# Hybrid decoder trunk on one core: other places for the first token tiles, the first gate tile and the narrow projections

## The chip, the cores and the metric

The kernel runs on one core of one Trainium2 chip. The metric is the device time of one execution in microseconds (us). The engines are named as the profile names them: PE is TensorE's matmuls and PEld its weight loads, DVE is VectorE, ACT is ScalarE, POOL is GpSimd, SP issues DMAs. Matrix products land in PSUM, which has eight banks; everything else on the chip is SBUF.

## The reference, cut to what matters

The model is one layer: a mixer with two branches (gated linear attention, "gla", and "mlstm"), each with four heads, and a gated feed-forward block with a causal convolution. 16 learned tokens stand ahead of 1024 input tokens, so the sequence has T = 1040 rows of 1024 channels.

```python
h = concat([meta, x])                      # 1040 x 1024
n = rms_norm(h, norm_mix)
proj = n @ w_in + b_in                     # q, k, v, gate r, 16 low-rank columns for gla;
                                           # q, k, v, gate o, 4 + 4 columns (i, f) for mlstm; gates a, b
log_a = log_sigmoid(g_lr @ gla_w_gate + gla_b_gate) / 16
o_gla = head_rms(gla(q, k, v, log_a)) * silu(r)
o_ml  = head_rms(mlstm(conv(q, k), v, i, f)) * sigmoid(o)
h = h + (sigmoid(a) * (o_gla @ w_gla) + sigmoid(b) * (o_ml @ w_ml)) @ w_out
h = h + conv_ffn(rms_norm(h, norm_ffn))
return rms_norm(h, norm_final)[16:]
```

## The kernel before, in words

Every float32 product is made of three products of split operands: a matrix X is held as a rounded part XH and a rest XL, and XH·WH, XL·WH and XH·WL are summed in PSUM. Splitting costs one copy on ACT (the H part) and one subtraction on DVE (the L part).

**The token tiles.** `load_x` (line 291) loads tile 0 (the 16 meta tokens) and tiles 1 to 8 (128 tokens each) by SP into SBUF slots with tags "w" (tiles 0 to 4), "q" (5, 6) and "k" (7, 8), slots that the heads use later. `norm_x(i)` (line 299) takes a tile's sum of squares on ACT (L305), makes the reciprocal root on DVE and POOL (L308, L310), scales the tile by it and by the norm's vector `gmix` on DVE (L311), transposes it on PE in two groups of four (L316, PSUM tag "s", three banks) and splits it into xH (ACT, L318) and xL (DVE, L320). Lines 323 to 341 write out the order of these loads, norms and first weights by hand.

**The weights.** `Units` holds a list of weight pieces in the order of use. `get(u)` loads and splits the pieces up to two ahead of u (the first three without looking ahead). `prep` (line 96) loads a piece into one of two raw slots by SP, copies on ACT (L102) and subtracts on DVE (L103) into a ring of three slots each for H and L. Before, unit 0 is the key of head 0 (gk), 1 the query (gq) and 2 the narrow projections "lr": the 16 low-rank columns of gla and the 4 + 4 of mlstm, padded to 128 in two zeroed tiles that take one slot of each ring (line 106). `prep_small` loads them with three DMAs.

**The products.** `proj_cm` (line 146) multiplies a weight piece of 128 columns with the tokens, piece of tokens by piece: 24 products (8 blocks of channels, 3 each) into one of three PSUM banks with tag "pj", and then a copy out by ACT that adds the bias from `col`. `TH_ALL` and `TH_POST` cut the tokens into three pieces of some 342 ("thirds" below), `SEG_ALL` and `SEG_POST` into four of some 256, whose borders fall on token tiles. For head 0 the key, the query and lr go piece by piece in turn (`together`, line 403), so that products start with tiles 0 to 2. `proj_v` makes the values in nine pieces of 24 or fewer products. `columns()` (line 282) transposes the rows of biases and other vectors in `va` into `col`; it stands ahead of the last token tile. `conv_columns()` does the same for the feed-forward's convolution; it stands behind head 0's projections.

**The order after the start.** `main(gen)` runs the main work, and after each piece `advance()` runs one step of the side chain, up to its next `yield`. Stage s (lines 863 to 870) appends head s to the side chain (and `small_rows` behind head 0, which needs lr's rows), and then does as main work the gate projection of head s (two tiles, six thirds; copy out at L426), the key, query and value of head s + 1 (15 pieces) and one gate of the merge (three). A head's side chain ends with four pairs of chunks (L716 to L727) and `post` (line 510): a scale per token (L92, L520), the gate's activation (L518), transposes (L530, L537), the product with the gate tile (L532, L538), the split and two stores (L540 to L543), for each of two halves. The gate tiles have tag "r" with two slots, so that a gate tile of head s + 1 can be written only when `post` of head s has read the one before it.

**How an order comes about.** Each instruction has a priority, which is its place in the program; `hp(n)` moves it up by n places, though not ahead of `floor`, which is set behind the start. At compile time each engine's order is fixed from these priorities and from what is ready in the compiler's own model of time; on the chip each engine then works strictly in that order.

Of the kernel before, what the change touches and what calls it, by code (L numbers as in the profile page):

```python
# [16 lines left out]
P = 128  # L17
D = 1024
NM = 16
SEQ = 1024  # L20
T = NM + SEQ
NK = D // P
NP = SEQ + 2
T0 = NM - 2
NC = SEQ // P
# [19 lines left out]
def hybrid_kernel(ctx, tc, x, meta, norm_mix, w_in, b_in, gla_w_gate, gla_b_gate, gla_norm,  # L45
# [7 lines left out]
    def rowb(ap, off, n):  # L53
        return bass.AP(tensor=ap.tensor, offset=ap.offset + off, ap=[[0, P], [1, n]])
# [3 lines left out]
    def hp(n):  # L58

        return tc.high_priority(offset=max(1, min(n, tc.cur_priority - floor[0])))  # L60
# [42 lines left out]
        nc.vector.tensor_tensor(wL, raw, wH.bitcast(F32), OP.subtract)  # L103
        return wH, wL

    lrHL = [wp.tile([P, NK, P], F32R, name=f"w{p}_lr", tag="w" + p) for p in "HL"]
    for t in lrHL:
        nc.vector.memset(t.bitcast(F32), 0.0)
    SMALL = ((0, O_LR, 16), (32, O_MI, 4), (64, O_MF, 4))

    def prep_small():
# [92 lines left out]
    def u_cm(w, n0, name):  # L204
        return U.add(wsrc(w, 0, NK, n0, P), [P, NK, P], name)
# [7 lines left out]
    def head_units(s):  # L213
        h = s % 4
        if s < 4:
            uk[s], uq[s] = u_cm(w_in, O_GK + P * h, f"gk{h}"), u_cm(w_in, O_GQ + P * h, f"gq{h}")
            if s == 0:
                uk["lr"] = U.add()
            uv[s] = u_v(O_GV + DV * h, f"gv{h}_")
        else:  # L220
            uk[s], uq[s] = u_cm(w_in, O_MK + P * h, f"mk{h}"), u_cm(w_in, O_MQ + P * h, f"mq{h}")
            uv[s] = u_v(O_MV + DV * h, f"mv{h}_")

    def gate_units(s):
        h = s % 4
        o = (O_GR if s < 4 else O_MO) + DV * h
        ur[s] = [u_cm(w_in, o + P * j, f"r{s}_{j}") for j in range(2)]

    head_units(0)
    for s in range(8):  # L230
# [51 lines left out]
    def columns():  # L282

        tp = ps.tile([P, 512], F32, name="coltp", tag="s", bufs=3)
        nc.tensor.transpose(tp[:, :nrow], va[:nrow, :], ident[:nrow, :nrow])
        nc.vector.tensor_copy(col, tp[:, :nrow])
        nc.vector.tensor_scalar(col[:, C_GQ:C_GQ + 4], col[:, C_GQ:C_GQ + 4], QS, None, OP.mult)

    xts = []

    def load_x(*tiles):
        for i in tiles:
            n = NM if i == 0 else P
            tag, bufs = [("w", 5), ("q", 2), ("k", 2)][(i >= 5) + (i >= 7)]
            xt = hd.tile([P, T], F32, name=f"xt{i}", tag=tag, bufs=bufs)
            nc.sync.dma_start(xt[:n, :D], meta if i == 0 else x[P * (i - 1):P * i, :])
            xts.append(xt)

    def norm_x(i):
        n = NM if i == 0 else P  # L300
        c0 = 0 if i == 0 else NM + P * (i - 1)
# [3 lines left out]
        nc.scalar.activation(junk[:n, :D], xt[:n, :D], AF.Square, accum_out=ss[:n])  # L305
        with hp(40):
            v = hd.tile([P, 1], F32, name=f"xv{i}", tag="xv", bufs=3)
            nc.vector.tensor_scalar(v[:n], ss[:n], 1.0 / D, EPS, OP.mult, OP.add)  # L308
            rs = hd.tile([P, 1], F32, name=f"xr{i}", tag="xr", bufs=3)
            last = nc.gpsimd.tensor_tensor(rs[:n], v[:n], mhalf[:n], OP.pow)  # L310
        nc.vector.scalar_tensor_tensor(xt[:n, :D], xt[:n, :D], rs[:n], gmix[:n], OP.mult, OP.mult)  # L311
        for g in range(2):
            tp = ps.tile([P, 4, P], F32, name=f"xtp{i}_{g}", tag="s", bufs=3)
            for j in range(4):
                k = 4 * g + j
                nc.tensor.transpose(tp[:, j, :n], xt[:n, k * P:(k + 1) * P], ident[:n, :n])  # L316
            h4 = xH[:, 4 * g:4 * g + 4, c0:c0 + n]
            nc.scalar.activation(h4, tp[:, :, :n], AF.Copy)  # L318
            l4 = xL[:, 4 * g:4 * g + 4, c0:c0 + n]
            nc.vector.tensor_tensor(l4, tp[:, :, :n], h4.bitcast(F32), OP.subtract)  # L320
        return last

    load_x(0)
    nc.sync.dma_start(gmix, rowb(norm_mix, 0, D))
    load_x(1, 2)
    norm_x(0)
    norm_x(1)
    U.get(0, 0)
    load_x(3)
    U.get(1, 0)  # L330
    norm_x(2)
    load_x(4, 5)
    U.get(2, 0)
    norm_x(3)
    load_x(6, 7, 8)
    for dst, ap in small:
        nc.sync.dma_start(dst, ap)
    for i in range(4, NC + 1):
        if i == NC:
            columns()  # L340
        last = norm_x(i)
    for t, c in ((xH, 0), (xL, 32)):
        m3 = xM[:, :48 * NK].rearrange("p (k w) -> p k w", w=48)
        nc.scalar.activation(m3[:, :, c:c + NM], t[:, :, :NM].bitcast(F32), AF.Copy)
    floor[0] = tc.cur_priority

    fc = const.tile([P, 4, 44], F32, name="fc")

    def conv_columns():
        for i in range(2):  # L350
            tp = ps.tile([P, 512], F32, name=f"ftp{i}", tag="s", bufs=3)
            nc.tensor.transpose(tp[:, :88], vf[:, i, :], ident[:88, :88])
            nc.vector.tensor_copy(fc[:, 2 * i:2 * i + 2, :].rearrange("p a b -> p (a b)"), tp[:, :88])

    def cc(i):
        return col[:, i:i + 1]
# [32 lines left out]
    def head_proj(s):  # L389
        h = s % 4  # L390
        hh = heads[s] = {}
        bB = hd.tile([P, DV], F32, name=f"bB{s}", tag="bB", bufs=2)
        nc.sync.dma_start(bB, rowb(b_in, (O_GV if s < 4 else O_MV) + DV * h, DV))
        kT = hd.tile([P, T + 3], F32, name=f"kT{s}", tag="k", bufs=2)
        qT = hd.tile([P, T + 3], F32, name=f"qT{s}", tag="q", bufs=2)
        hh["k"], hh["q"] = kT, qT
        if s < 4:
            pk = proj_cm(uk[s], TH_ALL if s else SEG_ALL, 0, lambda p, t0, n: nc.scalar.activation(
                kT[:, t0:t0 + n], p, AF.Identity, bias=cc(C_GK + h)))
            pq = proj_cm(uq[s], TH_POST if s else SEG_POST, T0, lambda p, t0, n: nc.scalar.activation(  # L400
                qT[:, t0:t0 + n], p, AF.Identity, bias=cc(C_GQ + h), scale=QS))
            if s == 0:
                yield from together(pk, pq, proj_cm(uk["lr"], SEG_ALL, 0, lambda p, t0, n: nc.scalar.activation(
                    raw_s[0:96, t0:t0 + n], p[0:96, :], AF.Identity, bias=bsm[0:96])))
            else:
                yield from pk
                yield from pq
        else:
            for z, u, c in ((kT, uk[s], C_MK), (qT, uq[s], C_MQ)):
                nc.gpsimd.memset(z[:, 0:3], 0.0)  # L410
                yield from proj_cm(u, TH_ALL, 0, lambda p, t0, n, z=z, c=c: nc.scalar.activation(
                    z[:, 3 + t0:3 + t0 + n], p, AF.Identity, bias=cc(c + h)))
# [6 lines left out]
    def gate_proj(s):  # L419
        hh = heads[s]  # L420
        hh["r"] = []
        for j in range(2):
# [3 lines left out]
            yield from proj_cm(ur[s][j], TH_POST, T0, lambda p, t0, n, r=r, c=c: nc.scalar.activation(  # L426
                r[:, t0:t0 + n], p, AF.Identity, bias=cc(c)))

    def merge_gate(which, j):
# [427 lines left out]
    def main(gen):  # L857
        for _ in gen:
            advance()

    main(head_proj(0))
    conv_columns()
    for s in range(8):
        side.append((gla if s < 4 else mlstm)(s))
        if s == 0:
            side.append(small_rows())
        main(gate_proj(s))
        if s < 7:
            main(head_proj(s + 1))
        main(merge_gate("a", s))  # L870
# [565 lines left out]
```

## Time and profile before

| | |
|---|---|
| median of 3 runs | 1974.15 us (1971.41 to 1975.38) |
| profiled execution | 1973.3 us, of which the profile's span is 1971.4 us |
| PE busy | 1936.3 us, 98% of the span |
| DVE, ACT, POOL busy | 49%, 38%, 15% |
| DMA | 224.82 MB, mean 114 GB/s |

A row of the timeline gives start, duration, engine, line, operation, names (written <- read), the shapes, how many instructions are merged, and in brackets the idle time of the engine just before with what ended it. A row of the list of waits gives the waiting engine and line, whom it waited for, the total in us, how often and the longest. A row of the windows gives for each stretch its length and each engine's busy time with the number of instructions, then the granted clock of TensorE, the DMA engines' share and GB/s. The order of the engines there is PE, PEld, DVE, ACT, POOL. A busy time of PE includes the modelled end of a pipelined product, so that products follow each other closer than their durations say.

### The profile page before, as it was taken

The numbers are of one execution on the slowest core, as the hardware profiler recorded it, in microseconds if no ns is written. First come the engines' busy times: TensorE is split into PE (matmuls) and PEld (weight loads), VectorE is DVE, ScalarE is ACT, GpSimd is POOL, SyncE is SP. The second block draws the span as 40 slices with busy tenths as digits, with TensorE's granted clock in tenths as the row PEclk, the third lists the DMA queues.
The fourth block names the chain that finished last, engine by engine and source line by source line (L and its number), as shares of the span: only waits on it lengthen the run. The fifth ranks groups of instructions, "written<-read, shape, count | busy, mean of one in ns | idle before, by whom it ended". The sixth has DMA issues, their size and how long they took to land. (4 is left out here: it accounts for less than half of the span.)

```text
span 1971.4 us, 31346 instructions
## 1 busy us (share of the span) xinstructions
PE 1936.3 (98%) x13333; PEld 1854.0 (94%) x13333; DVE 963.4 (49%) x1427; ACT 744.3 (38%) x1176; POOL 286.5 (15%) x201
## 2 busy tenths in 40 slices
PE   7999999999999999999999999999999999999998
PEld 6999999999999999999999999999999999978886
DVE  6265263637535343422022446698888888710202
ACT  5145333535534343423221234544545444431211
POOL 2020020101000000000000002012222222364220
PEclk9999999999999999999999999999999999999999
DMA  4210403232234222226971433333333333487731
GB/s 152 57 33 23 100 22 95 37 70 69 61 96 90 64 88 63 79 62 123 315 268 54 150 108 108 124 102 126 116 119 123 118 118 113 170 301 263 239 101 43
DMA packets 191271, 224.82 MB, mean 114 GB/s; under 512 B 11102, under 2 KB 150640, under 8 KB 191131
## 3 DMA queue, kind: packets, MB, share of 16 engines
q1 hardware_dynamic: 190843, 221.76, 37.2%
q8 instruction: 105, 1.72, 0.4%
q10 hardware_dynamic: 288, 1.05, 0.1%
q14 instruction: 35, 0.29, 0.0%
HBM read 166.07 MB, written 56.71 MB: 113 GB/s over the span
## 5 line engine op out<-in xcount | busy, mean ns | idle before, releaser
L1323 PE MATMUL pd<-ringH,a 128*128 128x512 f32 x416 | 131.6, 393 | 1.5 <-DMA a<-adrL 1.5
L154 PE MATMUL pj<-xH,wH_r 128*128 128x342 f32 x384 | 124.2, 323 | 0.4 <-ACT r L426 0.4
L154 PE MATMUL pj<-xH,wL_r 128*128 128x342 f32 x384 | 122.9, 320 | 0.0
L154 PE MATMUL pj<-xL,wH_r 128*128 128x342 f32 x384 | 122.5, 319 | 0.0
L1357 DVE TENSOR_TENSOR acc<-pd,acc 128x512 f32<-128x512 f32 x16 | 11.1, 692 | 196.3 <-PE pd L1323 196.3
L1323 PEld LDWEIGHTS pd<-ringH,a 128*128 128x128 f32 x416 | 78.0, 188 | 19.6 <-DMA a<-adrL 2.0
L1323 PE MATMUL pd<-ringL,a 128*128 128x512 f32 x208 | 82.5, 397 | 1.5 <-POOL ringL L1302 1.5
L197 PE MATMUL pv<-wH_gv,xH 128*128 128x256 f32 x256 | 75.4, 294 | 0.0
L197 PE MATMUL pv<-wH_mv,xH 128*128 128x256 f32 x256 | 74.2, 290 | 0.0
L1193 PE MATMUL po<-wL_wo,yH 128*128 128x256 f32 x256 | 72.0, 282 | 2.0 <-DVE wL_wo L103 2.0
L1193 PE MATMUL po<-wH_wo,yH 128*128 128x256 f32 x256 | 72.8, 284 | 0.9 <-DVE h L1200 0.9
L154 PEld LDWEIGHTS pj<-xH,wH_r 128*128 128x128 f32 x384 | 72.2, 188 | 1.1 <-ACT r L426 0.5
L627 POOL TENSOR_TENSOR pk<-pk,kT 128x512 f32<-128x512 f32 x24 | 40.2, 1685 | 226.9 <-ACT pk L626 226.8
L197 PE MATMUL pv<-wL_gv,xH 128*128 128x256 f32 x256 | 72.7, 284 | 0.0
L197 PE MATMUL pv<-wH_gv,xL 128*128 128x256 f32 x256 | 72.6, 283 | 0.0
L154 PEld LDWEIGHTS pj<-xL,wH_r 128*128 128x128 f32 x384 | 72.2, 188 | 0.0
L154 PEld LDWEIGHTS pj<-xH,wL_r 128*128 128x128 f32 x384 | 72.2, 188 | 0.0
L197 PE MATMUL pv<-wL_mv,xH 128*128 128x256 f32 x256 | 71.9, 281 | 0.0
L197 PE MATMUL pv<-wH_mv,xL 128*128 128x256 f32 x256 | 71.9, 281 | 0.0
L1193 PE MATMUL po<-wH_wo,yL 128*128 128x256 f32 x256 | 71.8, 281 | 0.0
L1154 DVE SCALAR_TENSOR_TENSOR cv<-u,fc,cv 128x1024 f32<-128x1024 f32 x44 | 69.4, 1578 | 0.4
L201 DVE TENSOR_TENSOR v<-pv,bB 128x256 f32<-128x256 f32 x64 | 27.0, 421 | 78.1 <-PE pv L197 77.9
(618 smaller groups left out, 6714.5 us busy)
## 6 DMA issues: line engine op xcount, KB each, us to landing
rd<-in_ffn_w_down_dram SPq DMA_DIRECT2D x36, 512.0 KB, 5.9
rg<-in_ffn_w_up_dram SPq DMA_DIRECT2D x22, 512.0 KB, 4.2
ru<-in_ffn_w_up_dram SPq DMA_DIRECT2D x22, 512.0 KB, 3.8
a<-adrH SPq DMA_DIRECT2D x44, 256.0 KB, 5.0
a<-adrL SPq DMA_DIRECT2D x44, 256.0 KB, 4.7
adrH<-aH SPq DMA_DIRECT2D x21, 512.0 KB, 2.6
adrL<-aL SPq DMA_DIRECT2D x21, 512.0 KB, 2.6
wr_r<-in_w_in_dram SPq DMA_DIRECT2D x16, 512.0 KB, 4.0
```

The source lines that it names most:

```text
L154: nc.tensor.matmul(pt[:, :n], a[:, k, :], b[:, k, base + t0:base + t0 + n], start=(i == 0), stop=(i == 3 * NK - 1))
L197: nc.tensor.matmul(pt[:, :DV], a[:, k, t0:t0 + P], b[:, k % 4, :], start=(i == 0), stop=(i == 3 * NK - 1))
L201: nc.vector.tensor_tensor(vt[:n, c, :DV], pt[:n, :DV], bB[:n, :], OP.add)
L627: nc.gpsimd.tensor_tensor(pe, pe, lv(kv, b)[:, :, 0, :], OP.mult)
L1154: nc.vector.scalar_tensor_tensor(y, u[:, j:SEQ + j], fc[:, j, jj:jj + 1], y, OP.mult, OP.add)
L1193: nc.tensor.matmul(pt[:, :DV], a, b[:, k % 4, :], start=(k == 0 and i == 0), stop=(k == NK - 1 and i == len(terms) - 1))
L1323: nc.tensor.matmul(pts[t][n], a[:, c], b[:, 512 * n:512 * n + 512], start=start and i == 0, stop=stop and i == 2)
L1357: nc.vector.tensor_tensor(acc[:, h], pts[t][n], acc[:, h], OP.add)
```

## The change

- The first two token tiles are loaded ahead of `gmix`. Tile 3 is loaded behind the weights of gk and gq; five of the rows that `col` needs come behind it, four others go at the very top on ACT's own DMA queue, and the rest behind tile 8.
- `columns()` moves ahead of tile 3's norm, `conv_columns()` behind tile 8's.
- Unit 2 is now the first gate tile's weights (r0_0). Its projection takes the place of lr in `together`, in four pieces; lr follows behind it in thirds. In stage 0 only the second gate tile is left of the gate projection.
- The padded narrow weights lie in one tile in a slot of tag "v" and no longer in the weights' rings. Token tiles 5 and 6 share the other slot of "v", tile 7 has a slot of "k", tile 8 one of "q".
- Tile 1's transposes use the "pj" banks, and each tile's split (L318, L320) has a priority of 40.
- Eight products of the identity with itself, whose result nobody reads, stand at the top.

```diff
-    lrHL = [wp.tile([P, NK, P], F32R, name=f"w{p}_lr", tag="w" + p) for p in "HL"]
-    for t in lrHL:
-        nc.vector.memset(t.bitcast(F32), 0.0)
+    lr2 = hd.tile([P, 2, NK, P], F32R, name="w_lr", tag="v", bufs=2)
+    nc.vector.memset(lr2.bitcast(F32), 0.0)
+    lrHL = [lr2[:, i] for i in range(2)]
...
             if s == 0:
+                ur[0] = [u_cm(w_in, O_GR, "r0_0")]
                 uk["lr"] = U.add()
...
-            tag, bufs = [("w", 5), ("q", 2), ("k", 2)][(i >= 5) + (i >= 7)]
-            xt = hd.tile([P, T], F32, name=f"xt{i}", tag=tag, bufs=bufs)
+            if i in (5, 6):
+                if i == 5:
+                    x56.append(hd.tile([P, 2, D], F32, name="xt56", tag="v", bufs=2))
+                xt = x56[0][:, i - 5]
+            else:
+                tag, bufs = ("w", 5) if i < 5 else ("k", 2) if i == 7 else ("q", 2)
+                xt = hd.tile([P, T], F32, name=f"xt{i}", tag=tag, bufs=bufs)
...
-            tp = ps.tile([P, 4, P], F32, name=f"xtp{i}_{g}", tag="s", bufs=3)
+            tp = ps.tile([P, 4, P], F32, name=f"xtp{i}_{g}", tag="pj" if i == 1 else "s", bufs=3)
...
+            with hp(40):
+                h4 = xH[:, 4 * g:4 * g + 4, c0:c0 + n]
+                nc.scalar.activation(h4, tp[:, :, :n], AF.Copy)
+                l4 = xL[:, 4 * g:4 * g + 4, c0:c0 + n]
+                nc.vector.tensor_tensor(l4, tp[:, :, :n], h4.bitcast(F32), OP.subtract)
...
+    def idle_products(n, name):
+        pt = ps.tile([P, P], F32, name=f"idle{name}", tag="ot", bufs=2)
+        for _ in range(n):
+            nc.tensor.matmul(pt, ident, ident, start=True, stop=True)
+
+    idle_products(8, "a")
+    for dst, ap in small[:4]:
+        nc.scalar.dma_start(dst, ap)
+    load_x(0, 1)
+    nc.sync.dma_start(gmix, rowb(norm_mix, 0, D))
+    load_x(2)
+    norm_x(0)
+    norm_x(1)
+    U.get(0, 0)
+    U.get(1, 0)
+    norm_x(2)
+    load_x(3)
+    for dst, ap in small[4:9]:
+        nc.sync.dma_start(dst, ap)
+    load_x(4, 5)
+    U.get(2, 0)
+    columns()
+    norm_x(3)
+    load_x(6, 7, 8)
+    norm_x(4)
+    for dst, ap in small[9:]:
+        nc.sync.dma_start(dst, ap)
+    for i in range(5, NC + 1):
+        last = norm_x(i)
+    conv_columns()
...
-                yield from together(pk, pq, proj_cm(uk["lr"], SEG_ALL, 0, lambda p, t0, n: nc.scalar.activation(
-                    raw_s[0:96, t0:t0 + n], p[0:96, :], AF.Identity, bias=bsm[0:96])))
+                yield from together(pk, pq, gate_proj(0, (0,)))
+                yield from proj_cm(uk["lr"], TH_ALL, 0, lambda p, t0, n: nc.scalar.activation(
+                    raw_s[0:96, t0:t0 + n], p[0:96, :], AF.Identity, bias=bsm[0:96]))
...
-        main(gate_proj(s))
+        main(gate_proj(s, (0, 1) if s else (1,)))
```

The lines that the second part of the diff replaces (323 to 341 before) load tile 0, `gmix`, tiles 1 and 2, then norm tiles 0 and 1, get gk, load tile 3, get gq, norm tile 2, load tiles 4 and 5, get lr, norm tile 3, load tiles 6 to 8 and all the rows, and norm the rest.

More of the change, by code (lines that the diff above doesn't have):

```diff
@@ L226, in gate_units @@
         o = (O_GR if s < 4 else O_MO) + DV * h
-        ur[s] = [u_cm(w_in, o + P * j, f"r{s}_{j}") for j in range(2)]
+        ur.setdefault(s, []).extend(u_cm(w_in, o + P * j, f"r{s}_{j}") for j in range(len(ur.get(s, ())), 2))
     head_units(0)
@@ L287, in columns @@
         nc.vector.tensor_scalar(col[:, C_GQ:C_GQ + 4], col[:, C_GQ:C_GQ + 4], QS, None, OP.mult)
-    xts = []
+    xts, x56 = [], []
     def load_x(*tiles):
@@ L316, in norm_x @@
                 nc.tensor.transpose(tp[:, j, :n], xt[:n, k * P:(k + 1) * P], ident[:n, :n])
[L317 to L320, printed above, removed]
-        return last
[L323 to L345, printed above, removed]
+            with hp(40):
[3 more added lines that the diff above has]
+                nc.vector.tensor_tensor(l4, tp[:, :, :n], h4.bitcast(F32), OP.subtract)
+        return last
     fc = const.tile([P, 4, 44], F32, name="fc")
@@ L353, in conv_columns @@
             nc.vector.tensor_copy(fc[:, 2 * i:2 * i + 2, :].rearrange("p a b -> p (a b)"), tp[:, :88])
+    def idle_products(n, name):
[27 more added lines that the diff above has]
+    conv_columns()
+    for t, c in ((xH, 0), (xL, 32)):
+        m3 = xM[:, :48 * NK].rearrange("p (k w) -> p k w", w=48)
+        nc.scalar.activation(m3[:, :, c:c + NM], t[:, :, :NM].bitcast(F32), AF.Copy)
+    floor[0] = tc.cur_priority
     def cc(i):
@@ L417, in head_proj, with gate_proj @@
         yield from proj_v(uv[s], bB, vt)
-    def gate_proj(s):
+    def gate_proj(s, js=(0, 1)):
         hh = heads[s]
-        hh["r"] = []
-        for j in range(2):
+        hh.setdefault("r", [])
+        for j in js:
             r = hd.tile([P, NP], F32, name=f"r{s}_{j}", tag="r", bufs=2)
@@ L425, in gate_proj @@
             hh["r"].append(r)
-            yield from proj_cm(ur[s][j], TH_POST, T0, lambda p, t0, n, r=r, c=c: nc.scalar.activation(
+            yield from proj_cm(ur[s][j], TH_POST if s or j else SEG_POST, T0, lambda p, t0, n, r=r, c=c: nc.scalar.activation(
                 r[:, t0:t0 + n], p, AF.Identity, bias=cc(c)))
@@ L861, in hybrid_kernel @@
     main(head_proj(0))
-    conv_columns()
     for s in range(8):
```

## The prediction, made before the changed kernel ran

> **What bounds the kernel now.** I read the page first: busy shares, then the idle column of TensorE's groups, then the list of waits for that engine, and only then the start in order of time.
>
> ```profile
> PE 1936.3 (98%) x13333; PEld 1854.0 (94%) x13333; DVE 963.4 (49%) x1427; ACT 744.3 (38%) x1176; POOL 286.5 (15%) x201
> ```
>
> TensorE is busy 98% of 1971.4 us, so the time is its work plus its holes. The waits, and the 5 us windows of the start (the last three columns: granted clock, DMA share, GB/s), say where holes are. The fifth row is ScalarE's, and (f) needs it:
>
> ```profile
> PE xtp L316 <- DVE xt L311: 10.4, 2, 10.0
> PE ot L530 <- DVE or L520: 1.6, 1, 1.6
> PE pj L154 <- ACT r L426: 0.4, 1, 0.4
> PE pj L154 <- ACT kT L398: 0.4, 1, 0.4
> ...
> ACT r L426 <- DVE of L538: 32.6, 5, 10.9
> ...
> 5.00:10.00 5.00, 0.02 (x1) 0.02 (x1) 2.05 (x16) 2.30 (x4) 1.77 (x2) 1.00 1.03 367
> ...
> 15.00:20.00 5.00, 2.74 (x15) 2.07 (x16) 5.00 (x10) 4.95 (x11) 1.10 (x2) 0.83 0.87 236
> 20.00:25.00 5.00, 5.00 (x24) 5.00 (x24) 4.59 (x10) 2.79 (x5) 2.52 (x3) 0.50 0.34 124
> ```
>
> Ten microseconds pass before anything can be transposed, VectorE is full from 15 to 20, and from 20 to 25 TensorE runs at half the clock. After 37 us it hardly waits. So the change can win holes at the start, and lose where it makes new ones later; the work of TensorE stays. The first gate tile goes from three pieces to four and the narrow projection from four to three: 24 products more and 24 fewer over nearly the same columns, net nothing.
>
> **The start, step by step.** The rows that carry it:
>
> ```profile
> 1.26 0.41 SPq L324 DMA_DIRECT2D gmix<-in_norm_mix_dram  x1
> ...
> 7.36 1.06 ACT L305 ACTIVATE xj<-xt 128x1024 f32<-128x1024 f32 x1 [3.29 <-DMA xt<-in_x_dram]
> 8.65 1.27 DVE L311 SCALAR_TENSOR_TENSOR xt<-xt,xr,gmix 16x1024 f32<-16x1024 f32 x1
> ...
> 12.40 1.28 DVE L311 SCALAR_TENSOR_TENSOR xt<-xt,xr,gmix 128x1024 f32<-128x1024 f32 x1 [0.41 <-POOL xr L310]
> 16.00 1.27 DVE L311 SCALAR_TENSOR_TENSOR xt<-xt,xr,gmix 128x1024 f32<-128x1024 f32 x1
> 17.19 1.22 DVE L103 TENSOR_TENSOR wL_gq<-wr_gq,wH_gq 128x1024 fp32r<-128x1024 f32 x1
> 18.99 0.68 DVE L320 TENSOR_TENSOR xL<-xtp,xH 128x512 fp32r<-128x512 f32 x1
> 19.83 0.57 PE L154 MATMUL pj<-xL,wH_gk 128*128 128x272 f32 x1
> ...
> 24.74 0.43 PE L154 MATMUL pj<-xL,wH_gk 128*128 128x272 f32 x1
> ...
> 30.59 0.29 PE L154 MATMUL pj<-xH,wH_lr 128*128 128x272 f32 x1
> ...
> 32.98 0.28 PE L154 MATMUL pj<-xL,wH_lr 128*128 128x272 f32 x1
> 33.20 1.07 PE L316 MATMUL xtp<-ident,xt 128*128 128x128 f32 x8
> ```
>
> (a) Tile 1 lands at 7.36 behind gmix. 512 KB at 367 GB/s is 1.4 us, so with their places exchanged tile 1 lands near 5.9 and gmix near 7.4. VectorE's scaling (L311) needs both; it waited for tile 1's sum of squares until 8.65 and will wait for gmix: 1.3 us earlier. Tile 2's scaling follows (12.40 becomes about 11.1). Then comes the larger part: between 12.40 and the last low part of tile 2 (18.99, end 19.67) VectorE also did tile 3's scaling (1.27) and wL_gq (1.22). With a priority of 40 the low parts go ahead of these, and tile 1's transposes leave tag "s" for "pj", so tile 2 waits for no bank. 19.67 - 1.3 - 2.5 = 15.9; I take 16.3 for the first sustained product instead of 19.83, since ScalarE works in order and may stand behind the cast of gq, bounds 15.2 and 18. Of the 3.5 us, tile 3's eight transposes (1.1, the row at 33.20) fall back into the products' time: -2.4.
>
> (b) The first pieces of kT could not leave PSUM before `col` was made:
>
> ```profile
> 34.60 0.29 PE L154 MATMUL pj<-xH,wL_lr 128*128 128x272 f32 x1
> 35.70 0.25 DVE L286 COPY col<-coltp 128x98 f32<-128x98 f32 x1
> 36.43 0.48 ACT L398 ACTIVATE kT<-pj,col 128x272 f32<-128x272 f32 x1
> 36.96 0.39 PE L154 MATMUL pj<-xH,wH_gk 128*128 128x256 f32 x1 [0.39 <-ACT kT L398]
> ```
>
> From 34.9 to 36.96 TensorE had only eight transposes (1.1): 1.0 us lost. Moving columns() ahead of tile 3, with its rows loaded early, and tiles 5 and 6 out of the "q" slots, ends that: -1.0. Next late there would be r0_0's weights, in need near 16.3 + 48 products = 23 to 25. Their load has to wait for the raw slot of gk (until wL_gk is made) and holds tiles 6 to 8 behind it on SP; these are used at 33 or later. Bubbles from this and from VectorE's row: +0.5, bounds 0 and 1.5.
>
> (c) At the half clock a product took 0.23 us (19.83 to 24.74, 21 steps), at the full one 0.126 (30.59 to 32.98, 19 steps): 23 products, 2.4 us lost. After, the products meet the same gate; I take 1.7 lost, bounds 0 and 3.4: -0.7.
>
> (d) Costed at nothing: four row loads on ScalarE's queue. SP paid 0.41 for an issue, so 1.6 us on ScalarE, which idles 3.29 us before 7.36; without that cover 1.6. Five more row loads stand on SP ahead of tile 4, 2.1 us of issuing, but the DMA engines are full (share 1.03 from 5 to 10 us) and drain behind SP; without that cover 2.1. The narrow weights' loads and casts move behind the tiles, and lr now comes after twelve pieces of 24 products, some 35 us on; its tile in slot "v" is read out before v0's first sum. The eight idle products: a plain float32 one is two instructions, and eight took 2.05 us at full clock (row at 339.13 below), 4.1 at half. They run at the very top, where TensorE has nothing else for 10.0 us (the first wait above).
>
> By the trace the clock fell after 1.55 us of idleness (below), so idle products that end well before the first transposes carry nothing to 16. The Trainium skill ("TensorE: Matmul & The Clock Gate", Part 1, the HAM clock gate) has the clock at half until some 3.4 us of sustained work, and back at half after an idle window of that length. That agrees on the products; on the idle length the trace is stricter, and by that rule alone the clock's share in (f) would cost nothing and the sum would be 0.9 lower.
>
> Sum at the start: -2.4 - 1.0 + 0.5 - 0.7 = **-3.6**, ends +0.8 (18, cold 3.4, bubbles 1.5) and -6.9 (15.2, no cold).
>
> **What the missing gate tile does to the order.** After each third of main work (24 products of 342 columns, or one v piece) one step of the side chain is issued. Stage 0 had 24 main steps (gate 6, next head 15, merge 3); after, 21. By their yields gla needs 23 side steps and small_rows 7, so everything up to head 3 comes three main steps later against main.
>
> (e) In stage 0 this helps:
>
> ```profile
> 183.36 1.93 DVE L520 TENSOR_SCALAR or<-or,rs0r 128x256 f32<-128x256 f32 x7 [1.19 <-POOL rs0r L92]
> 183.77 1.12 PE L530 MATMUL ot<-ident,or 128*128 128x128 f32 x4 [1.55 <-DVE or L520]
> ...
> 173.35:182.22 8.87, 8.87 (x74) 8.64 (x72) 6.46 (x5) 8.71 (x12) 2.82 (x2) 1.00 0.00 1
> 182.22:183.77 1.55, 0.00 (x0) 0.00 (x1) 0.41 (x2) 0.74 (x1) 1.10 (x1) 1.00 0.00 0
> 185.56:188.97 3.41, 3.41 (x19) 3.41 (x17) 3.28 (x7) 1.06 (x1) 0.00 (x0) 0.50 0.02 5
> ```
>
> Three v pieces (8.87 us) covered a chain of 10.4 and TensorE stood 1.55; then the clock was half for 3.41 us, 1.7 lost. After, one v piece and two thirds of ga stand there, 3.0 + 2 x 3.6 = 10.2 (a third's 3.6 comes under (f)): 0.2 is left and the clock stays, **-3.0**, or 0 if not.
>
> (f) At the start of stage 2 it hurts. A tile r2_0 takes the slot of r1_0, and its copies out of PSUM wait for head 1's post (L538):
>
> ```profile
> 308.07 0.59 PE L721 MATMUL op<-S,qh 128*128 128x256 f32 x2
> ...
> 312.51 2.56 DVE L520 TENSOR_SCALAR or<-or,rs1r 128x256 f32<-128x256 f32 x8 [1.79 <-POOL rs1r L92]
> 315.25 1.21 DVE L103 TENSOR_TENSOR wL_gk<-wr_gk,wH_gk 128x1024 fp32r<-128x1024 f32 x1
> 319.80 0.60 PE L530 MATMUL ot<-ident,or 128*128 128x128 f32 x4
> 324.01 0.60 PE L530 MATMUL ot<-ident,or 128*128 128x128 f32 x4
> 324.65 0.75 DVE L532 SCALAR_TENSOR_TENSOR of<-ot,col,r 128x512 f32<-128x512 f32 x1 [3.45 <-PE ot L530]
> 326.45 0.21 DVE L538 SCALAR_TENSOR_TENSOR of<-otm,col,r 128x2 f32<-128x2 f32 x1
> 326.72 0.22 PE L537 MATMUL otm<-ident,om 2*128 2x2 f32 x1 [0.61 <-DVE of L538]
> 326.75 1.42 ACT L426 ACTIVATE r<-pj,col 128x342 f32<-128x342 f32 x3 [1.65 <-DVE of L538]
> 339.13 2.05 PE L564 MATMUL sc<-qT,kT 128*128 128x128 f32 x16 [0.17 <-DVE of L532]
> ```
>
> Before, four thirds lay between the last chunk pair (308.7) and L538 (326.45), and all three "pj" banks were full: it just fitted, with 0.61 + 0.4 us of holes. After, one third is left there (two of r2_0 are done already). Without main work in its way the chain takes from 308.7 to 316.5 (scaling and wL_gk), two L532 and L538 (1.7), the copy out (0.55): 10.1 us. The cover is one third (4.21 from one group of transposes to the next, less 0.60: 3.6), sixteen transposes (2 x 1.1) and two small ones (0.4): 6.2. A hole of 3.9, 2.9 more than now. 1.7 for the clock counts half, since the transposes break the hole up: **+3.7**, bounds 0 (the scheduler fills it) and 7.0 (a chain of 12.5, the clock in full). Behind the waiting copies ScalarE holds the cast for head 1's second half, which L538 there needs 13 us later, as now.
>
> (g) Stage 3 has two thirds, 9.8 of cover against 10.1, stage 4 three: **+0.3**, bounds 0 and 4.4 (12.5 and the clock).
>
> Sum: -3.6 - 3.0 + 3.7 + 0.3 = -2.6. The profiled execution took 1973.3 (span 1971.4 and 1.9 around it), so 1970.7; the median of the runs, 1974.15, is 0.85 higher: **1971.5**.
>
> **The rivals**, all on the median's scale.
> - No new hole: TensorE's thirds and the side chain settle otherwise and (f), (g) stay away, with the old 1.0 gone: -3.6 - 3.0 - 1.0 = -7.6, 1966.6. For it: 0.4 us of waiting on L426 in all now. Against: ScalarE already idles 32.6 us there for L538, so the slack is used.
> - Slower: the chain behind the last chunk pair takes 12.5 us rather than 10.1, as it can where casts come between (in stage 0 it took 10.4 to the first transpose alone). Then stage 2 holds 5.3 + 1.7 and stage 3 2.7 + 1.7: -6.6 + 11.4 = +4.8, 1978.9; from a chain of 12.1 us on it is slower.
> - The start doesn't move: ScalarE stands behind late weights, start 0: -3.0 + 4.0 = +1.0, 1975.2.
> - The idle products do hold the full clock to the first products: (c) -2.4 instead of -0.7, 1969.8. The Trainium skill's rule on the idle window (same page and section) speaks against it, as the trace does.
>
> **How the numbers follow.** About 0.2% (3.9 us) is what a measurement here tells from no change: faster is under 1970.2, slower over 1978.1. Forecast 0.42 (its own range 1968 to 1976), no new hole 0.30, slower 0.15, unmoved start 0.08, held clock 0.05. Faster: 0.30 + 0.05 = 0.35; same 0.42 + 0.08 = 0.50; slower 0.15. The range runs from a start at its better end without a hole (a little under 1966) to past the slower rival: 1964.5 to 1980.
>
> **What would show it.** Right: tile 1's squares before 6.5, sustained products from about 16, no wait of L154 for kT; no hole near 180; a wait of L154 for L426 of 2 to 5 us where head 2's gate begins. Wrong: products from 18 or later, holes between 20 and 50 us over 2, or waits for L426 at every head.

## The result: 0.48% slower, and the profile after

The changed kernel takes 1981.8 us (median of 6 runs, 1980.19 to 1984.41) against 1971.64 of the kernel before (6 runs): a ratio of 1.0048, 95% interval 1.0035 to 1.0061, or 7 to 12 us more. The forecast was 1971.5, 2.6 us under the 1974.15 of the three runs of before that were known then, and its range ended at 1980. The profiled execution took 1981.92, its span is 1980.1 (before: 1971.4).

The lines of after (the code has moved: L446, L540, L550, L552, L558 and L606 are L426, L520, L530, L532, L538 and L586 of before). First the page's busy line:

```profile
PE 1943.4 (98%) x13349; PEld 1857.9 (94%) x13349; DVE 961.8 (49%) x1426; ACT 744.1 (38%) x1175; POOL 285.0 (14%) x201
```

TensorE's work is the same but for 16 instructions, the idle products. They are 3.8 of the 7.1 us that its busy time is longer; the other 3.3 have no work of their own. That fits the mean granted clock, 0.994 against 0.996 before. The list of waits of TensorE in after, and one row of ScalarE's (total, times, longest):

```profile
PE ot L550 <- DVE of L552: 4.5, 6, 1.1
...
PE pj L154 <- ACT r L446: 2.6, 3, 1.0
...
PE ot L550 <- DVE or L540: 1.9, 2, 1.1
...
PE sc L606 <- DVE pk L648: 1.5, 2, 1.3
...
PE sc L606 <- POOL pk L647: 0.4, 1, 0.4
```

```profile
ACT r L446 <- DVE of L558: 39.2, 6, 10.8
```

Before, the list had 1.6 us for `or` and 0.4 for `r`, with 0.6 in the small transposes. Now there are waits at the ends of heads 0 to 3 and at the scores behind them (`sc`), in all 10.9 us. The wait of 10 us at the top is shorter in part only because idle products fill it up to 5.6 us. The start in order of time, in three views of after (ScalarE, VectorE, TensorE):

```profile
5.08 1.06 ACT L311 ACTIVATE xj<-xt 128x1024 f32<-128x1024 f32 x1 [1.02 <-DMA xt<-in_x_dram]
```

```profile
7.16 2.47 DVE L317 SCALAR_TENSOR_TENSOR xt<-xt,xr,gmix 16x1024 f32<-16x1024 f32 x2 [0.75 <-POOL xr L316]
...
13.88 2.48 DVE L327 TENSOR_TENSOR xL<-xtp,xH 128x512 fp32r<-128x512 f32 x4 [0.25 <-ACT xH L325]
```

```profile
1.82 3.79 PE L342 MATMUL idlea<-ident 128*128 128x128 f32 x16 [1.82 <-POOL ident masks.py:199]
...
14.87 0.59 PE L154 MATMUL pj<-xH,wH_gk 128*128 128x272 f32 x1 [0.20 <-ACT xH L325]
15.27 0.42 PE L154 MATMUL pj<-xH,wH_gq 128*128 128x258 f32 x1
15.82 0.59 PE L154 MATMUL pj<-xL,wH_gk 128*128 128x272 f32 x1
...
19.37 0.36 PE L154 MATMUL pj<-xH,wH_gk 128*128 128x272 f32 x1
19.57 0.29 PE L154 MATMUL pj<-xL,wH_gk 128*128 128x272 f32 x1
```

Tile 1's squares come at 5.08 (7.36 before), the low parts of tiles 1 and 2 in one piece at 13.88, sustained products from 15.82 (19.83). At 5 to 10 us the DMA engines are as full as before (share 1.05 below). At 19.5 the spacing of the products goes from 0.23 to 0.125 us: there the clock becomes full. The windows of after (columns as before: PE, PEld, DVE, ACT, POOL, clock, DMA share, GB/s), three of the start and two of later half-clock stretches:

```profile
5.00:10.00 5.00, 1.59 (x13) 1.20 (x13) 3.49 (x19) 2.30 (x4) 1.10 (x2) 0.93 1.05 321
...
15.00:20.00 5.00, 4.86 (x22) 4.55 (x23) 4.25 (x9) 3.84 (x8) 1.79 (x2) 0.55 1.00 371
20.00:25.00 5.00, 5.00 (x45) 5.00 (x45) 4.37 (x6) 3.44 (x7) 0.15 (x1) 1.00 0.48 161
...
255.04:258.45 3.41, 3.41 (x18) 3.41 (x18) 3.41 (x5) 0.73 (x1) 1.51 (x1) 0.50 0.17 50
326.72:330.13 3.41, 3.41 (x14) 3.06 (x13) 1.10 (x1) 2.28 (x4) 0.00 (x0) 0.50 0.62 190
```

So the first products come as forecast, even a little sooner, and the loss lies between 180 and 600 us. The first product of gate b (wH_gb), behind which both kernels are alike, starts at 881.75 before and at 889.58 after: 7.8 of the span's 8.7 us are lost by then.

### The profile page after: what moved, and what is told of

It is laid out like the page before. It is cut to its first block, busy times and chain, and to the rows that moved or that the text cites. A ratio compares the mean times of both kernels' runs of the same rounds, so it can differ in the third digit from the quotient of the medians.

```text
span 1980.1 us, 31382 instructions
## 1 busy us (share of the span) xinstructions
PE 1943.4 (98%) x13349; PEld 1857.9 (94%) x13349; DVE 961.8 (49%) x1426; ACT 744.1 (38%) x1175; POOL 285.0 (14%) x201
## 3 DMA queue, kind: packets, MB, share of 16 engines
q10 hardware_dynamic: 352, 1.07, 0.1%
## 5 line engine op out<-in xcount | busy, mean ns | idle before, releaser
L154 PE MATMUL pj<-xH,wH_r 128*128 128x342 f32 (+2 forms) x392 | 126.8, 323 | 0.7 <-ACT r L446 0.7
L154 PE MATMUL pj<-xH,wL_r 128*128 128x342 f32 (+2 forms) x392 | 124.6, 318 | 0.0
L154 PE MATMUL pj<-xL,wH_r 128*128 128x342 f32 (+2 forms) x392 | 124.4, 317 | 0.0
L154 PEld LDWEIGHTS pj<-xH,wH_r 128*128 128x128 f32 x392 | 74.2, 189 | 1.7 <-ACT r L446 1.0
L154 PEld LDWEIGHTS pj<-xL,wH_r 128*128 128x128 f32 x392 | 74.2, 189 | 0.2
L154 PEld LDWEIGHTS pj<-xH,wL_r 128*128 128x128 f32 x392 | 74.2, 189 | 0.0
L154 PE MATMUL pj<-xH,wH_ga 128*128 128x342 f32 x192 | 63.6, 331 | 0.0
```

What stands on the lines that cost most here:

```text
L154: nc.tensor.matmul(pt[:, :n], a[:, k, :], b[:, k, base + t0:base + t0 + n], start=(i == 0), stop=(i == 3 * NK - 1))
```

## The experiments

**Theory:** stage 0 lost three main pieces, so every side chain up to head 3 stands three pieces late against main work (the lag). Each head's end then has less cover, that is, less main work for TensorE to do while the chain of that end runs. That costs about 12 us; the start wins 2 to 5. **Rivals:** the loss comes from the new start itself (tile order, idle products, priorities, lr in another place), or from extra steps wherever they are put. "Ratio" is that of the runs to those of before on the same chip, with its 95% interval.

**1. Lag undone, crowded.** The changed kernel with two side steps behind each of stage 0's three gate pieces.

```diff
-        main(gate_proj(s, (0, 1) if s else (1,)))
+        if s == 0:
+            for _ in gate_proj(0, (1,)):
+                advance()
+                advance()
+        else:
+            main(gate_proj(s))
```

> The changed kernel, with two side steps instead of one behind each of the three gate pieces of stage 0, so that the side chain has its 24 steps there again. Theory A (the start gains about 4.4 us, and the three missing side steps cost about 12 at the gate tiles of heads 1 to 4): the 12 goes and the time is 3 to 5 us under the kernel before, with TensorE's waits for L446 and for L552 back under 1.5 us in all. Theory B (the loss comes from the new places of the weights and slots, not from the count of steps): still 7 to 10 us over the kernel before.

Measured: 1975.83, ratio 1.0021 [1.0013, 1.0030]; 6 us under the changed kernel, but still slower than before: between the figures of the two theories. The waits for the gate tiles are back to 0.4, and two new ones stand at 110 and 114, where the crowded steps are (its TensorE waits):

```profile
PE sc L606 <- POOL pk L647: 1.5, 1, 1.5
...
PE sc L606 <- DVE pk L648: 0.8, 1, 0.8
```

A half-clock stretch follows there (116.64 to 120.05). The lag is real, and a step that comes too early has a price too.

**2. Lag alone.** The kernel before, with the first three gate pieces of stage 0 left without a side step. Nothing of the start is in it.

```diff
-        main(gate_proj(s))
+        for n, _ in enumerate(gate_proj(s)):
+            if s or n >= 3:
+                advance()
```

> The kernel before, with no side step behind the first three gate pieces of stage 0, and nothing else changed. Theory A: 9 to 13 us slower than the kernel before, with new waits of TensorE behind the gate tiles of heads 2 to 4. Theory B: within 2 us of the kernel before.

Measured: 1983.99, ratio 1.0063 [1.0051, 1.0075], +12.4 us. Its TensorE waits are those of after, nearly row for row (the third stands at 2.6 there):

```profile
PE ot L530 <- DVE of L532: 4.5, 6, 1.1
...
PE ot L530 <- DVE or L520: 1.9, 2, 1.1
PE pj L154 <- ACT r L426: 1.9, 2, 1.4
...
PE sc L586 <- DVE pk L628: 1.5, 2, 1.3
```

This shows the cause: the lag by itself, with the old start, costs no less than the whole change does.

**3. Lag undone, spread.** The changed kernel with one extra side step behind every seventh of stage 0's 21 main pieces.

```diff
...
-        main(gate_proj(s, (0, 1) if s else (1,)))
+        if s == 0:
+            for g in (gate_proj(0, (1,)), head_proj(1), merge_gate("a", 0)):
+                for _ in g:
+                    advance()
+                    ahead[0] += 1
+                    if ahead[0] % 7 == 0:
+                        advance()
+            continue
+        main(gate_proj(s))
```

> The changed kernel, with three extra steps of the side chain spread evenly over stage 0 (one behind each seventh of its 21 pieces) instead of crowded behind the first three. Theory A (the three-step lag of the side chain against the main work is what costs, and it costs about 12 us; the start itself wins about 4): from stage 1 on every step stands where it stood before the change, and in stage 0 no place carries two extra steps in a row, so the waits for the gate tiles' copies (L446) and the later holes go and no new ones come near 110: the median is 9 to 11 us under the changed kernel's, 1970 to 1973. Rival B (an extra step costs wherever it is put, because the piece behind it is too short for its chain): no better than the variant with the crowded steps, 1975 to 1977.

Measured: 1972.03, ratio 1.0001 [0.9992, 1.0010], 9.8 us under the changed kernel's median. The crowded variant's extra waits are absent; TensorE's waits for the heads' ends are those of before again:

```profile
PE ot L550 <- DVE or L540: 1.6, 1, 1.6
...
PE otm L557 <- DVE of L558: 0.6, 1, 0.6
...
PE pj L154 <- ACT r L446: 0.4, 1, 0.4
```

With experiment 2 this holds the lag from both sides: 12.4 us when added to the old kernel, 9.3 (the ratios' difference) when taken from the new one. Whether the 3 us between them are more than the intervals, about 2 us each way, stays open.

**4. and 5. One and six pieces of lag.** As experiment 2, with `n >= 1` and `n >= 6`.

> The kernel before, with no side step behind the first of stage 0's six gate pieces (three were left out in the lag alone, which cost 12.3 us): the side chain stands one main piece late from there on. Theory A in its simple form (each piece of lag takes some 4 us of cover from every end of a head, and the cost is linear): a third of 12.3, 1975 to 1977. Rival G (the chains have slack of about one piece, and the cost comes past a threshold): within 1.5 us of before, 1970 to 1973, with the waits for the gate tiles' copies as before.

> The kernel before, with no side step behind any of stage 0's six gate pieces: six pieces of lag instead of three. Theory A, linear: twice 12.3, 1995 to 1998. Rival H (past the slack every further piece of lag is paid in full at each of the six ends of a head that follow, about 3.6 us each time and three pieces more): 12.3 + up to 65, 2020 to 2050. Rival I (the compiler puts other work into the holes, and the cost saturates): 1984 to 1990.

Measured: one piece 1973.74, ratio 1.0010 [1.0001, 1.0019], +2.0 us; six pieces 2013.01, ratio 1.0210 [1.0196, 1.0224], +41.4. Neither the linear forms nor the saturation fit, and full payment of every further piece is just missed: 1, 3 and 6 pieces cost 2, 12 and 41 us, that is 2.0 for the first, 5.2 for each of the next two, 9.7 for each of the last three. The first piece is cheap, and from there on the price of a piece rises. The waits for `or` show it: with three pieces they are 1.07 and 0.84 us, at the ends of heads 0 and 1; with six they are 4.6, 4.6 and 7.0, at the ends of heads 1 to 3. With six, the waits of TensorE and the windows of its half-clock stretches are:

```profile
PE ot L530 <- DVE or L520: 16.2, 3, 7.0
...
PE ot L530 <- DVE of L532: 4.6, 5, 2.3
PE sc L586 <- DVE pk L628: 4.1, 3, 2.1
```

```profile
210.46:220.70 10.24, 6.55 (x23) 6.07 (x24) 3.98 (x7) 4.71 (x7) 0.65 (x1) 0.50 0.47 137
...
579.10:592.75 13.65, 9.11 (x34) 7.89 (x35) 7.35 (x17) 6.40 (x8) 2.87 (x2) 0.50 0.31 92
sum 47.78, PE 38.99 PEld 34.86 DVE 26.98 ACT 18.24 POOL 6.54; mean PE 6.50 PEld 5.81 DVE 4.50 ACT 3.04 POOL 1.09
```

The six half-clock stretches (first, last and the sum are shown) hold 39.0 us of products, so 19.5 us are lost to the clock alone, beside some 25 of waiting (16.2 + 4.6 + 4.1). Together 44 us, less the 5 of before: nearly the 41 measured. Behind the longer holes the half clock comes on top, for 3.41 to 13.65 us at a time.

**6. Start alone.** The changed kernel with lr back in turn with key and query, and both gate tiles in stage 0: the new tile order, rows, priorities and idle products without the lag.

```diff
-                yield from together(pk, pq, gate_proj(0, (0,)))
-                yield from proj_cm(uk["lr"], TH_ALL, 0, lambda p, t0, n: nc.scalar.activation(
-                    raw_s[0:96, t0:t0 + n], p[0:96, :], AF.Identity, bias=bsm[0:96]))
+                yield from together(pk, pq, proj_cm(uk["lr"], SEG_ALL, 0, lambda p, t0, n: nc.scalar.activation(
+                    raw_s[0:96, t0:t0 + n], p[0:96, :], AF.Identity, bias=bsm[0:96])))
...
-        main(gate_proj(s, (0, 1) if s else (1,)))
+        main(gate_proj(s))
```

> The changed kernel with the narrow projections back beside key and query and both gate tiles back in stage 0: all other parts of the change stay (loads, columns, slots, priority, idle products). Theory A: 3 to 5 us under the kernel before, since stage 0 has its 24 side steps. Theory B: slower than before by most of the 10 us.

Measured: 1970.92, ratio 0.9990 [0.9982, 0.9999]: faster, by 2 us and not by the 3 to 5 expected, with an interval that only just leaves out 1. The start is no rival cause of the loss: 12.4 for the lag less these 2 is the 10 of the whole change.

**7. and 8. Without idle products, and without the priority.** The start alone, with the call of `idle_products` left out; and then also with `hp(1)` in place of `hp(40)` at the tiles' split.

> The start alone (both gate tiles in stage 0, lr back in the turn with key and query), without the eight idle products. Theory C (the idle products bring a warm clock from 6 to 9 us that nothing uses, and the window that follows them makes the first real products cold as long as before; they give nothing): within 1 us of the start alone with them, 1970 to 1972. Rival D (the clock's windows start from the first activity of TensorE, and with the idle products its first rise comes sooner behind the first sustained product): the products are cold 1 to 3 us longer, so 0.5 to 1.5 us slower than with them, 1971.5 to 1972.5. Rival E (they cost something): 1 us or more faster, under 1970.

> The start alone without idle products, and with each tile's split (copy and subtraction) at a priority of 1 instead of 40. Step (a) of the forecast (the priority takes tile 3's scaling and the low part of gq out of the way of tile 2's low part, 2.5 us): the first sustained product comes 2 to 3 us later than with the priority, and the time is 1 to 2.5 us longer than the start alone without idle products, 1971 to 1973. Rival (the order on VectorE comes out the same without it): within 0.7 us, 1969 to 1970.5.

Measured: 1969.56, ratio 0.9989 [0.9980, 0.9998]; and 1969.58, ratio 0.9986 [0.9977, 0.9995]. The idle products give nothing: against before on the same chip the ratio is 0.2 us from that of the start alone, though the time by itself, 1969.56, would lie in rival E's range. Their removal does move the products: sustained ones start at 17.46 rather than 15.88, but the clock is full at 19.06 rather than 20.07, and the first product of head 0's values (L184) starts at 59.40 against 58.67. The priority gives nothing in the end either: without the priority as well, the sustained products start at 17.30 and those values at 58.69. The time is the rival's, though not for its reason, as the order on VectorE does differ (see (a) below).

**9., 10. and 11. The narrow rows' steps elsewhere.** `small_rows` appended behind head 3 instead of head 0, in the changed kernel (`if s == 3:` for `if s == 0:`, label rows_late) and in the start alone (start_rows_late); and put behind the eighth step of head 3, in the start alone without idle products (start_rows_mid; `amid` runs the rows' steps behind that step).

```diff
...
-        side.append((gla if s < 4 else mlstm)(s))
-        if s == 0:
-            side.append(small_rows())
+        head = (gla if s < 4 else mlstm)(s)
+        side.append(amid(head, small_rows(), 7) if s == 3 else head)
...
```

> The changed kernel with the side chain of the narrow rows (small_rows, 7 steps) appended behind head 3 instead of behind head 0. Heads 1 to 3 then come seven steps earlier against main. Theory A: all waits for gate tiles go, the kernel before's own too; 5 to 9 us under the kernel before. Theory B: still 7 to 10 us over it.

> The start alone, with the seven steps of small_rows appended behind head 3 instead of behind head 0, so that heads 1 to 3 stand seven steps earlier against the main work than before. Theory A (holes near the heads' ends come from a side chain too late against the main work): the 0.6 and 0.4 us waits at 325 to 327 go as well, and the time is 1 to 3 us under the start alone, 1968 to 1970, unless small_rows collide with a head's post, as they did in the changed kernel moved the same way (one hole of 3.16 us and the half clock behind it, 3.4 together). Rival (they collide here too): 1971 to 1974, with a hole of about 3 us near 510.

> The start alone without idle products, with the seven steps of small_rows in the middle of head 3 (behind its eighth step) instead of behind head 0. Theory J (the waits at a head's end where `or` waits for the power on GpSimd, 1.55 us near 180 and 3.16 us near 512, come from small_rows' scans on VectorE beside a head's post; away from any post they go, and heads 1 and 2 stand seven steps earlier): no hole near 180, 322 or 512, and 2 to 5 us under the start alone without idle products, 1965 to 1968. Rival (the work meets something else there, or the holes are the post's own): 1969 to 1972.

Measured: 1971.83, ratio 0.9999 [0.9991, 1.0008]; 1970.43, 0.9987 [0.9978, 0.9996]; 1970.45, 0.9989 [0.9980, 0.9998]. In the changed kernel seven steps less in front of heads 1 to 3 take back 10 us, as much as the lag had cost and not the 5 to 9 more of theory A. Where there is no lag they give nothing, for a collision goes where the rows go: a scan of theirs on VectorE runs beside the power on GpSimd that a head's `post` needs. The timeline of start_rows_late near 512, GpSimd and VectorE:

```profile
511.57 3.79 POOL L92 TENSOR_TENSOR rs3r<-rs3v,mhalf 128x9 f32<-128x9 f32 x1 [7.22 <-DVE rs3v L90]
```

```profile
511.26 0.16 DVE L90 TENSOR_SCALAR rs3v<-ss 128x9 f32<-128x9 f32 x1
511.45 2.32 DVE L482 TENSOR_TENSOR_SCAN sr<-rmask,sr 4x1040 f32<-4x1040 f32 x1
515.39 0.88 DVE L538 TENSOR_SCALAR or<-or,rs3r 128x256 f32<-128x256 f32 x3 [1.62 <-POOL rs3r L92]
```

TensorE waits 3.2 us there in place of 1.6 near 180. In the third variant the holes near 180, 322 and 512 are gone, as expected, and one of 2.5 us stands near 479, where the products for the values wait for a copy of the query on ScalarE, and two of 1.5 together near 545; the time is its rival's. In these variants a shift of the side chain by seven steps traded one hole for another.

**12. The kernel before, a second profile.**

> The kernel before, unchanged, for a second profile. Theory F (the stretch from the first product of the gate b's merge to the end, where the kernels are identical, varies by some us between executions, by the phase of the clock's windows and by DMA): that stretch differs from the first profile's 1089.7 us by 1 to 4 us. Rival (it repeats within 0.5 us): then the start alone, which took 1093.8 us there, lost 4 us to something systematic that the start left behind.

Measured: 1971.14 (one run), span 1969.4. From the first product of gate b to the end it takes 1092.2 us, against 1089.7 in the first profile: 2.5 us apart. Profiles of one kernel differ by that much, so the 1093.8 of the start alone is no sure loss that the start left behind. The windows of this second look at the place of step (e) and at 20 us:

```profile
180.36:181.91 1.55, 0.00 (x1) 0.00 (x0) 0.41 (x2) 0.74 (x1) 1.11 (x1) 1.00 0.00 0
181.91:190.00 8.09, 8.09 (x56) 7.53 (x57) 7.90 (x17) 2.12 (x2) 0.00 (x0) 1.00 0.02 4
```

```profile
20.00:25.00 5.00, 5.00 (x39) 5.00 (x39) 4.31 (x10) 3.73 (x11) 2.28 (x3) 1.00 0.36 123
```

The same wait of 1.55 us is there, and no half clock follows it. At 20 us the clock is full from 21.04 on, where the first profile had it only from 25.14. (The column shows 1.00 for the first microsecond too, because this profile's record of the clock begins at 21.04; the products' spacing of 0.23 us until then shows the half clock.) So both clock terms of the forecast rest on the luck of one execution.

A third slot for the gate tiles, or a second one for `of`, would have tested the slots directly; no run did.

## Why the prediction was wrong, point by point

**(a) Tile order: right in the number, in part by luck.** Products from 15.82, forecast 16.3. The exchange of places did its part: the scaling starts at 7.16, and 8.65 less 1.3 was forecast. The 2.5 us of the priority are not shown. Without idle products the low part of gq stands ahead of tile 2's low parts on VectorE, with the priority (15.46) and without it (15.09), and sustained products start at 17.46 and 17.30. Only with the idle products, which the forecast put at nothing, do tile 2's low parts go first, as in after. Neither was needed for what the start was worth in the end (experiments 7 and 8); which of its other parts brings that, no run separated.

**(b) The wait for kT: right.** No row of L154 waiting for kT is left. From 20 to 50 us TensorE idles 0.45 us in all, 0.74 before: 0.3 won, where -1.0 and +0.5 were forecast.

**(c) The cold clock: wrong sign.** In the old start five profiles have sustained products from 19.9 and the full clock at 25.14, 21.04, 22.71, 21.73 and 22.72, on the mean 2.8 us later. In the new start with idle products six have 15.8 and 19.52, 20.07, 19.34, 21.86, 20.31 and 21.07, on the mean 4.5 us later. Half of each is lost: 1.4 before, 2.3 after, +0.9 instead of -0.7. The forecast read its "before" from the profile with the longest cold stretch of the five. Against that one profile it came out: 3.7 us of half clock in the profile of after are 1.85 lost, forecast 1.7. The Trainium skill ("TensorE: Matmul & The Clock Gate", Part 1, the HAM clock gate) has the window of 3.4 us free-running, so that the same kernel warms up after a different time in each execution; these rows bear it out.

**(d) What was costed at nothing** cost nothing that shows: five variants of the new start have ratios of 0.9986 to 0.9990, on the mean 2.3 us faster than before. The first product of head 0's values agrees: 58.7 to 59.6 in those five, 60.8 to 62.6 in five with the old start, 2.5 us on the mean. The sum at the start was -3.6; it is -2.3, and the 1.6 by which (c) is off cover the difference.

**(e) to (g) The missing gate tile: here the forecast failed.** The waits in the traces and half of each half-clock stretch, before (first profile) and after:

| place | before | after | difference | forecast |
|---|---|---|---|---|
| head 0's end to head 1's scores, 180 to 256 | 1.55 + 1.7 | 1.07 + 0.68 + 1.29 + 1.7 | +1.5 | (e) -3.0 |
| head 1's end, 321 to 330 | 0.61 + 0.42 | 0.82 + 0.44 + 1.14 + 1.7 | +3.1 | (f) +3.7 |
| head 2's end, 379 to 456 | 0.47 | 0.38 + 0.31 + 1.14 + 0.94 | +2.3 | (g) +0.3 |
| head 3's end, 554 to 570 | 0 | 0.33 + 1.14 + 1.03 | +2.5 | (g) nothing |

The sum is +9.4 where +1.0 was forecast. Against the second profile of before, which has 2.6 us of waits and no half clock at these places, it is +11.5. With the start's -2.3 that makes +7.1 and +9.2: the measured 7 to 12. The step that failed is thus the bill of the lag. The forecast counted that every side chain comes three pieces late, but followed it to the old hole of (e) and to one chain at each of the next heads, and put the places behind these at nothing.

*(e)* said that one v piece and two thirds of ga would cover a chain of 10.4 us and that 0.2 would be left. The hole stayed, at 1.07, since the chain grew by a low part of weights that slips in between (after; GpSimd's power first, then VectorE):

```profile
183.58 3.81 POOL L92 TENSOR_TENSOR rs0r<-rs0v,mhalf 128x9 f32<-128x9 f32 x1 [5.59 <-DVE rs0v L90]
```

```profile
187.43 0.88 DVE L540 TENSOR_SCALAR or<-or,rs0r 128x256 f32<-128x256 f32 x3
188.22 1.22 DVE L103 TENSOR_TENSOR wL_r<-wr_r,wH_r 128x1024 fp32r<-128x1024 f32 x1
189.36 0.87 DVE L540 TENSOR_SCALAR or<-or,rs0r 128x256 f32<-128x256 f32 x3
```

And the late chain was followed for one place only. What hangs behind it came late as well: the second half's copy out (0.68 at 214.73) and head 1's first scores (1.29 at 251.99), which together are more than the hole that was to go. The 1.7 of the clock was booked as gone; a half clock came 70 us later instead.

*(f)* was right in place, and nearly in size by two errors against each other. It had a hole of 3.9 us as a wait of L154 for the gate tile, and half of the clock's 1.7. Measured are 2.4 us in three waits, all of the transposes and none of L154, and the whole 1.7. The timeline of after at head 1's end, TensorE and VectorE:

```profile
316.71 0.59 PE L741 MATMUL op<-S,qh 128*128 128x256 f32 x2
...
321.92 2.17 PE L550 MATMUL ot<-ident,or 128*128 128x128 f32 x8 [0.82 <-DVE or L540]
...
324.67 0.66 PE L550 MATMUL ot<-ident,or 128*128 128x128 f32 x4 [0.44 <-DVE of L552]
326.46 0.91 PE L550 MATMUL ot<-ident,or 128*128 128x128 f32 x4 [1.14 <-DVE of L552]
```

```profile
323.88 0.73 DVE L552 SCALAR_TENSOR_TENSOR of<-ot,col,r 128x512 f32<-128x512 f32 x1
324.55 1.20 DVE L103 TENSOR_TENSOR wL_gq<-wr_gq,wH_gq 128x1024 fp32r<-128x1024 f32 x1
325.68 0.73 DVE L552 SCALAR_TENSOR_TENSOR of<-ot,col,r 128x512 f32<-128x512 f32 x1
```

From the last pair (end 317.3) to L558 (end 326.5) the chain took 9.2 us; forecast were 9.5 to that point (10.1 with the copy out). The 1.14 is a low part of the next weights (L103) between two products with the gate; the same 1.14 stands at 441.49 and 555.72.

*(g)* counted a cover of two and three thirds at heads 2 and 3 against one chain of 10.1, found almost none missing, and counted no second half (for head 1's, (f) says "as now"). But the second half's chain starts when a store of the first half has landed, and at heads 2 and 3 the main work no longer reaches to the end of it (VectorE of after at head 3's end, then TensorE):

```profile
567.99 1.41 DVE L552 SCALAR_TENSOR_TENSOR of<-ot,col,r 128x512 f32<-128x512 f32 x2 [7.33 <-DMA oscgL<-of]
569.31 0.21 DVE L558 SCALAR_TENSOR_TENSOR of<-otm,col,r 128x2 f32<-128x2 f32 x1
```

```profile
570.23 0.43 PE L154 MATMUL pj<-xH,wH_mk 128*128 128x348 f32 x1 [1.03 <-ACT r L446]
```

The key's products for the next head wait for the gate tile that L558 has still to read. That is close to the third sign of "wrong" that the prediction named: waits for L446 stand at heads 0, 2 and 3, though not at head 1, the one place where it had forecast one. The slower rival had the right sign, but its mechanism, a chain of 12.5 us, is not what happened: the chain was a little shorter than forecast, and the loss was spread over four heads' ends, 1.5 to 3.1 us at each.

## What to carry to other kernels

When work is taken out of one stage of a kernel whose two streams run in lockstep, count the places that come late in every later stage until the streams are in step again, both halves of each, and not only the place with the old hole; a cheap test is to make the same lag in the old kernel by itself. Before shifting a whole side stream to remove one hole of a nearly full engine, look for the hole that it will open elsewhere: here each of three shifts made one. Read a clock term from more than one execution.

## What the runs showed of the hardware

**A wait of 1.55 us halves the clock in some executions and not in others; in eight profiles that goes with where it lies in a grid of 3.41 us.** In the first profile of before the clock changes at 18.31, 25.14, 185.56 and 188.97, whole multiples of 3.413 us apart (2, 47 and 1 of them). So it does in every profile here, from another starting point in each. The wait near 180 (178 to 185) stands in eight profiles. A half clock follows it in four (before, the start alone, its form without the priority, experiment 3); there it begins 0.1 to 1.0 us behind a line of this grid. None follows in the other four: in experiments 1 and 4 it begins 1.4 and 1.6 behind a line, and in the second profile of before and in the form without idle products a line cuts it in two. Why the place matters is not shown. Apart from the one at the kernel's very end, a later stretch at half speed always lasts 3.41 us or a multiple of it. In after it fell behind the waits at 251.99 (1.29) and 325.33 (1.14 with 0.44 ahead of it), and not behind those of 1.07 at 188.69 and 1.14 at 441.49 and 555.72. The Trainium skill (the section named under (c)) has the clock fall after an idle window of about 3.4 us; here far shorter waits did it.

**GpSimd's power of 9 elements takes twice as long beside a scan on VectorE.** It took 1.79 us at head 2 (timeline of GpSimd, after), 3.81 at head 0, where VectorE ran a scan over 1040 elements with two inputs in SBUF at the same time (183.47 to 185.79), and 3.79 in experiment 10. At head 3 of after it took 2.83, 1.04 more, beside a VectorE instruction of 1.30 us that reads two SBUF tiles (545.57). The row of head 2:

```profile
433.95 1.79 POOL L92 TENSOR_TENSOR rs2r<-rs2v,mhalf 128x9 f32<-128x9 f32 x1 [2.26 <-DVE rs2v L90]
```

The Trainium skill ("SBUF — State Buffer", "SBUF: two separate sides") has VectorE and GpSimd share a pair of ports that one instruction holds for its whole time, a VectorE one with two SBUF inputs among them. The trace agrees: the 2.0 us more are nearly the scan's 2.3.
